# Softmax attention on one core: a new order of the hand-written word lists, with the next batch's K sums later and one V load moved

## The chip, the cores and the metric

The kernel runs on one core of one Trainium2 chip. The metric is the device time of one execution in microseconds. Three runs of the kernel before took 792.56, 793.68 and 793.29, with a median of 793.29. The profile is of one more execution of the same program.

Engines are called by the names of the profile: PE is TensorE's matmuls, PEld its weight loads, DVE is VectorE, ACT ScalarE, POOL GpSimd and SP SyncE. POOL and SP only issue transfers here.

## The reference

```python
batch, seq_len, d_model = 8, 2048, 512
scores = np.matmul(q, k.transpose(0, 2, 1)) / np.sqrt(d_model)
attn_weights = special.softmax(scores, axis=-1).astype(np.float32)
return np.matmul(attn_weights, v)
```

All inputs and the output are float32. The kernel computes in float16 with float32 accumulation.

## The kernel before

**Two stages, both with seven products in place of eight.** Each batch has 2048 queries in two superblocks of 1024, and 2048 keys in 16 blocks, taken as 8 pairs `j`. For a superblock and a pair the 2 x 2 block product K times Q is made with Strassen's scheme (the Winograd form): seven products instead of eight, at the price of sums of the operands. Such a unit is a score *group* (class Group, lines 266 to 330). It is numbered through the whole kernel, so that group 48 is the first of the seventh superblock. Product n of a group is two matmuls of 512 columns. After it, ScalarE or VectorE empties or adds the bank: product 1 is copied to a second bank (L308), 5 and 6 are copied to SBUF (L312, L315), 7 and 3 are added there (L318, L321), 4 and 2 go through the exponential (L237). A further exponential takes the SBUF tile (the word `e`). The second stage multiplies the weights with V in the same way: a *pair* product (class Pair, L494) is eight matmuls of 256 or 257 columns, and a *leaf* product (class Leaf, L418) goes one level deeper, with eight matmuls of 128 columns, whose result VectorE adds to the output rows at once (L426).

**Sums.** VectorE makes the sums of operands: of K in `k_sums` (L185 to L188, four instructions for half a batch's keys), of Q in `q_sums` (L202 to L205), of V (L219 to L222 and L376 to L379), and of the weights (L352 to L355 for pairs, L395 to L398 for leaves). In K the second sum overwrites the raw block a21.

**The order is written by hand.** The kernel runs through 32 periods, four to a batch. A period is one string of words in `SEQUENCES` (lines 589 to 629), and each word issues its instructions on their engines at that place. Every engine takes its own instructions strictly in the order in which the words issue them, and waits at an instruction until its operands and its room are there. Periods 0, 1, 30 and 31 have strings of their own (`first`, `second`, `alone`, `last`); the others use the string of their number modulo 4, here called kind 0, 1, 2 and 3. Period 9 is thus of kind 1 and period 10 of kind 2. Kind 0 opens a batch of the second stage and kind 3 closes it. The score stage runs two periods ahead: kinds 0 and 1 score the batch's second superblock, and kinds 2 and 3 the next batch's first.

The words, with `'` for the period before:

- `.` is the next score product. QORDER (line 586) interleaves two groups: product 1 of this group, 7 of the one before, 5, 6, then 4 of the one before, 3, 2. `e` is the exponential of a finished SBUF tile.
- `a1` to `b7` are pair products of the tiles a and b; `L1` to `L7` are leaf products, of which L3 and L4 also scale and store rows (L435, L440 on SP).
- `xa0` to `xa3` are weight sums for the a tile of the next period, `xb0` to `xb3` for b of this one, and `ya0` to `ya3` the rest of a sum begun a period earlier (the last two of eight pairs in kind 2). `s1` to `s4` are leaf sums.
- `K00` is sum 0 of the next batch's first half of K, `K10`, `K20`, `K30` its sums 1 to 3; `K01` to `K31` are of the second half. `q0` to `q3` are sums of Q; `V..` of V, `w` and `u` of V's leaves.
- `lk2`, `lq3`, `lv1` load a chunk of K, Q or V of the next batch (POOL queue); `tk2`, `tq3` transpose a loaded chunk of K or Q by a transfer (SP queue, L146). Loads of K and Q share two stage buffers.

For the change these ties matter. K00 (into `ks1`) reads what tk0 and tk1 brought; its reader is product 5 of the next batch's first group (group 48 for periods 9 and 10). K20 is read by that group's product 6, K30 by product 3, K10 by product 7. q0 and q1 are read by products 5 and 6. The score banks are few: two for product 1 (`qx`), one each for its copy (`qy`) and for product 5 (`qz`); product 1 of a group takes the bank that product 4 of the group two before has left, once ScalarE has read it. One bank (`py`) serves the leaf products.

Of the kernel before, what the change touches and what calls it, by code (L numbers as in the profile page):

```python
# [12 lines left out]
def kernel(  # L13
# [561 lines left out]
    def pv(g, which):  # L575
# [3 lines left out]
        if which[1] == "1" and which[-1] != ">":  # L579
# [9 lines left out]
    SEQUENCES = {  # L589
        'first': (  # L590
# [4 lines left out]
        ),  # L595
# [4 lines left out]
        ),  # L600
# [4 lines left out]
        ),  # L605
# [4 lines left out]
        ),  # L610
        3: (
            "K11' a1 . . xa3' b7' . a5 xb0 . . L5' . e . L6' . s4' . . L3' s3' . . . L7' xb1 e xb2 "
            "xb3 a3 . . . b1 a6 e . . . a7 L4' s1 b5 xa0 . . L2 . s2 . . q0 xa1 L1 . . xa3 . . xa2 b3 "
            "q2 e q1 "
        ),
# [5 lines left out]
        ),  # L621
        'alone': (
# [1 line left out]
            "L4' xb2 a6 b3 xa2 a2 a7 b6 xa1 a4 xa3 b2 "  # L624
        ),
        'last': (
            "b7' q0 a1 a5 xb0 xb1 b4' a3 xb3 b1 b5 a6 b3 a2 xb2 b2 q1 b6 a7 b7 a4 q2 b4 "
        ),
    }

# [254 lines left out]
```

## Time and profile before

| what | value |
|---|---|
| median of three runs | 793.29 us |
| the profiled execution, own time | 789.77 us |
| its span, first to last instruction | 788.0 us |
| granted TensorE clock | 1.000 |
| busy share of the span: PE, DVE, ACT, POOL | 99%, 87%, 77%, 9% |
| DVE busy in periods 9, 10, 11, 12 | 21.57 of 24.00, 21.26 of 24.00, 19.00 of 23.90, 24.12 of 24.20 us |
| HBM traffic | 100.70 MB read, 33.55 MB written |
| one sum of 128 x 1024 in float16 on DVE | 0.68 us |
| a load of V, issue to landing, median | 9.8 us |

How to read it: all times inside the profile are counted from the span's start. A row of the timeline gives the start, the duration, the engine, the line of the kernel, the operation and its tiles; in brackets stands how long the engine was idle before, and what ended that. Matmuls overlap: a row's duration runs to the end of its pipeline, and the next may start before. What tells whether TensorE stands still is therefore the distance between starts.

### The profile page before, as it was taken

The page shows a single profiled execution, that of the slowest core. Times are in us where ns is not written, and L with a number is a line of the kernel's source. Part 1 is how long each engine was busy: PE and PEld are TensorE (multiplying, and loading weights), DVE is VectorE, ACT ScalarE, POOL GpSimd, SP SyncE. Part 2 cuts the span into 40 slices and gives each one's busy share as a digit, 9 for nine tenths or more (in the row PEclk, how much of TensorE's full clock was granted, in tenths as well). Part 3 has the DMA queues.
Part 4 walks back from the last instruction along what each step waited for, and adds up shares of the span by engine and source line. Part 5 has one row for each costly group of instructions (what it writes and reads, how often), then busy time and mean ns, then how long its engine had stood idle before and what let it go on. Part 6 is the DMA issues. An engine that isn't in the chain of part 4 may idle for free.

```text
span 788.0 us, 16301 instructions
## 1 busy us (share of the span) xinstructions
PE 783.1 (99%) x6284; PEld 536.5 (68%) x6284; DVE 685.4 (87%) x1452; ACT 610.4 (77%) x1140; POOL 71.7 (9%) x104
## 2 busy tenths in 40 slices
PE   9999999999999999999999999999999999999998
PEld 6566767667666666666766666666666766766687
DVE  5799988989889888998879988799897989889884
ACT  4888778787877878878787877878778787787762
POOL 4011100011000110010100001000110002000000
PEclk9999999999999999999999999999999999999999
DMA  9999995889958898489984989859996789911113
GB/s 220 183 167 133 183 188 110 166 145 164 180 120 162 155 172 166 97 161 180 170 158 110 159 161 183 160 103 174 155 203 123 124 172 147 202 54 46 48 66 111
DMA packets 187773, 115.90 MB, mean 147 GB/s; under 512 B 121520, under 2 KB 170800, under 8 KB 187696
## 3 DMA queue, kind: packets, MB, share of 16 engines
q0 software_dynamic: 49648, 49.29, 43.8%
q1 hardware_dynamic: 137616, 65.22, 36.1%
q8 instruction: 49, 0.80, 0.4%
q10 hardware_dynamic: 432, 0.36, 0.1%
q14 instruction: 28, 0.23, 0.1%
HBM read 100.70 MB, written 33.55 MB: 170 GB/s over the span
## 4 chain that ended last, share of the span: by engine, by line
PE 99%; DMA 0%; DVE 0%; issue 0%
PE t L298 47%; PE t L494 36%; PE t L418 12%; PE t L243 1%; PE t L258 1%; PE tr L156 1%; DMA rows<-in_q_dram 0%; PE t L768 0%; PE t L566 0%; DVE kraw L159 0%; DVE stage L135 0%; DVE rows L506 0%
## 5 line engine op out<-in xcount | busy, mean ns | idle before, releaser
L298 PE MATMUL t<-qraw,kraw 128*128 128x512 f16 x732 | 194.7, 379 | 0.0
L494 PEld LDWEIGHTS <-s 128*128 128x128 f16 x1536 | 148.3, 98 | 42.4 <-ACT rows L503 0.3
L298 PEld LDWEIGHTS <-kraw 128*128 128x128 f16 x984 | 93.0, 98 | 72.8 <-issue 0.3
L298 PE MATMUL t<-qs,ks 128*128 128x512 f16 x492 | 140.0, 379 | 0.0
L494 PE MATMUL t<-vt,s 128*128 128x257 f16 (+1 forms) x1024 | 132.9, 273 | 0.0
L237 ACT ACTIVATE right<-cz 128x1024 f16<-128x1024 f32 x123 | 130.1, 1058 | 1.9 <-DVE cz L318 1.9
L503 ACT ACTIVATE rows<-t,scales 128x256 f32<-128x256 f32 x136 | 63.9, 471 | 51.5 <-DVE scales L528 19.2
L426 DVE TENSOR_TENSOR rows<-t,rows 128x256 f32<-128x256 f32 x210 | 88.3, 420 | 15.5 <-PE t L418 8.1
L298 PEld LDWEIGHTS <-ks 128*128 128x128 f16 x738 | 68.7, 98 | 46.5 <-issue 0.4
L321 DVE TENSOR_TENSOR cz<-t,cz 128x512 f32<-128x512 f32 x123 | 84.4, 686 | 11.0 <-ACT cz L315 6.4
L237 ACT ACTIVATE left<-t 128x512 f16<-128x512 f32 x128 | 76.7, 600 | 20.2 <-PE t L298 16.4
L506 DVE SCALAR_TENSOR_TENSOR rows<-t,scales,rows 128x256 f32<-128x256 f32 (+1 forms) x134 | 63.9, 479 | 30.1 <-ACT rows L503 17.2
L318 DVE TENSOR_TENSOR cz<-t,cz 128x512 f32<-128x512 f32 x123 | 84.2, 684 | 5.1 <-PE t L298 5.1
L237 ACT ACTIVATE right<-t 128x512 f16<-128x512 f32 x138 | 83.0, 604 | 5.5 <-PE t L298 3.0
L312 ACT COPY cz<-t 128x512 f32<-128x512 f32 x122 | 71.5, 586 | 10.0 <-PE t L298 8.1
L315 ACT COPY cz<-t 128x512 f32<-128x512 f32 x123 | 71.8, 584 | 8.5 <-PE t L298 8.3
L418 PEld LDWEIGHTS <-left 128*128 128x128 f16 x960 | 62.6, 98 | 23.2 <-DVE left L398 3.8
L308 ACT COPY t<-t 128x512 f32<-128x512 f32 x121 | 69.8, 577 | 6.5 <-PE t L298 4.1
L298 PE MATMUL t<-qraw,ks 128*128 128x512 f16 x246 | 73.2, 379 | 0.0
L298 PE MATMUL t<-qs,kraw 128*128 128x512 f16 x246 | 73.2, 379 | 0.0
L494 PE MATMUL t<-vh,right 128*128 128x256 f16 x544 | 69.8, 273 | 0.0
L494 PEld LDWEIGHTS <-right 128*128 128x128 f16 x568 | 55.5, 98 | 17.5
(87 smaller groups left out, 1078.7 us busy)
## 6 DMA issues: line engine op xcount, KB each, us to landing
out_dram<-rows SPq DMA_DIRECT2D x60, 512.0 KB, 3.5
vh<-in_v_dram POOLq DMA_DIRECT2D x32, 512.0 KB, 9.8
stage<-in_q_dram POOLq DMA_DIRECT2D x28, 512.0 KB, 7.8
stage<-in_k_dram POOLq DMA_DIRECT2D x28, 512.0 KB, 6.7
right<-in_k_dram POOLq DMA_DIRECT2D x3, 512.0 KB, 11.8
out_dram<-rows SPq DMA_DIRECT2D x4, 256.0 KB, 2.0
out_dram<-rows SPq DMA_DIRECT2D x7, 128.0 KB, 1.7
rows<-in_q_dram SPq DMA_DIRECT2D x2, 256.0 KB, 3.2
```

The source lines that it names most:

```text
L237: nc.scalar.activation(out=out_, in_=in_, func=EXP, scale=inv_sqrt_d)
L298: nc.tensor.matmul(dst[:], lhs[:, j, dc, :], rhs[:, :, dc, :], start=(n in (1, 5) and dc == 0), stop=(dc == 1), skip_group_check=True,)
L308: self.edges[0](out=self.y[:], in_=self.x[:])
L312: self.edges[1](out=self.cz[:, 1, :], in_=self.z[:])
L315: nc.scalar.copy(out=self.cz[:, 0, :], in_=self.x[:])
L318: nc.vector.tensor_add(self.cz[:, 1, :], self.x[:], self.cz[:, 1, :])
L321: nc.vector.tensor_add(self.cz[:, 0, :], self.z[:], self.cz[:, 0, :])
L418: nc.tensor.matmul(to, lhs[:, j, h, :], rhs[:, j, :], start=(n in (1, 2) and h == 0 and j == 0), stop=(j == NK - 1), skip_group_check=True,)
L426: nc.vector.tensor_add(acc, part, acc)
L494: nc.tensor.matmul(dst[:, 0:width], lhs(j), rhs(j), start=(first and j == 0), stop=(j == NJ - 1), skip_group_check=True,)
L503: nc.scalar.activation(out=out_, in_=src, func=COPY, scale=r)
L506: nc.vector.scalar_tensor_tensor(out=out_, in0=src, scalar=r, in1=out_, op0=MULT, op1=ADD)
```

## The change

Only strings of `SEQUENCES` change; no instruction is added or taken away. In kind 1, K00, K20 and K30 move towards the end, and a7 and the products around it change places. The word `lv2` moves from kind 2, behind lq2, to the sixth place of kind 3, behind lv3. In kind 2, tk3 and tq3 are issued later, lq2 earlier in the string, and xb3, K01, K21, K31, q3, ya3, a3, b1 and L4' change places. Kinds 3 and 0, `first` and `last` have small exchanges of neighbours.

```diff
         'first': (
...
-            "za1 a5 v33 za3 . xb0 . . a3 v22 xb2 v21 . . lk0 v30 za2 . a6 . . v31 v32 xb1 tq1 . a7 . "
+            "za1 a5 v33 za3 . xb0 . . a3 v22 xb2 v21 . . lk0 v30 za2 . a6 . . v31 v32 xb1 . a7 tq1 . "
...
         1: (
             "a1 w3' . b7' . . L6' . w2' s4' . e L5' . . . s3' L3' a5 lk3 . xb0 xb1 . e . L7' xb3 . "
-            "tk1 a3 . . . xb2 a6 L4' . . . lk2 b1 . s1 K00 e K20 s2 a7 tk2 . lv1 . . L2 . b5 xa0 L1 . "
-            "q0 xa1 xa3 xa2 e . K30 . . b3 q2 q1 b6 . "
+            "tk1 a3 . . . xb2 a6 L4' . a7 lk2 . . b1 L2 . s1 e s2 . lv1 . . . b5 tk2 xa0 K00 . q0 K20 "
+            "L1 xa1 xa2 e . . b3 . q1 b6 . xa3 q2 K30 "
         ),
         2: (
-            ". . . b7' e K10' . L5' ya0 ya1 . tk3 . lq2 a1 lv2 . a5 ya3 q3 s3' L6' . . s4' ya2 . xb0 "
-            "e a3 . . L3' . xb1 xb2 a6 L7' K01 . lq3 tq3 K21 . a7 b1 xb3 . . . L4' b5 . L2 . s1 xa0 . "
-            "b3 xa2 e lv3 . tq2 K31 . s2 . b6 xa1 . L1 . . . e "
+            ". . . b7' e K10' . L5' ya0 ya1 lq2 a1 . tk3 . . a5 q3 ya3 s3' L6' . . s4' ya2 a3 . xb0 e "
+            ". . L3' . b1 xb1 xb2 a6 L7' xb3 K01 . lq3 . . . a7 L4' b5 K21 . . s1 xa0 tq3 . . L2 b3 "
+            "xa2 e lv3 . tq2 . s2 . b6 xa1 . L1 K31 . . . e "
         ),
         3: (
-            "K11' a1 . . xa3' b7' . a5 xb0 . . L5' . e . L6' . s4' . . L3' s3' . . . L7' xb1 e xb2 "
-            "xb3 a3 . . . b1 a6 e . . . a7 L4' s1 b5 xa0 . . L2 . s2 . . q0 xa1 L1 . . xa3 . . xa2 b3 "
-            "q2 e q1 "
+            "K11' a1 . . xa3' lv2 . a5 xb0 b7' . . L5' . e . L6' . s4' . . L3' s3' . . . L7' xb1 e "
+            "xb2 xb3 a3 . . . b1 a6 e . . . a7 L4' s1 b5 xa0 . . L2 . s2 . . xa1 L1 . q0 . xa3 . . "
+            "xa2 b3 q2 e q1 "
         ),
         0: (
...
-            "lk0 e L3' q3 xb1 V11 a3 . V21 . . xb2 L7' V31 lq1 V20 b1 . . . lv0 . V30 a6 ya2 . xb3 . "
-            "w0 u0 tk0 e . . L4' b5 xa0 w1 a7 u1 s1 . . u2 lk1 xa1 L2 . u3 b3 . xa3 b6 . . s2 L1 . e "
+            "lk0 e L3' q3 xb1 V11 a3 . V21 . xb2 . L7' V31 lq1 V20 b1 . . . lv0 . V30 a6 ya2 . xb3 . "
+            "w0 u0 tk0 e . . L4' b5 xa0 a7 u1 s1 . . u2 lk1 xa1 . L2 u3 b3 . w1 xa3 b6 . . L1 s2 . e "
             "xa2 tq1 "
         ),
...
         'last': (
-            "b7' q0 a1 a5 xb0 xb1 b4' a3 xb3 b1 b5 a6 b3 a2 xb2 b2 q1 b6 a7 b7 a4 q2 b4 "
+            "q0 b7' a1 a5 xb0 xb1 b4' xb3 a3 b1 b5 a6 b3 xb2 b2 a2 q1 b6 a7 b7 a4 q2 b4 "
         ),
```

## The prediction, as it was put on record

> **What bounds the kernel.** I read the totals first, then what TensorE waited for, then four periods of one batch side by side, then VectorE's waits, and last the places where a sum of K and the product that needs it stand in time.
>
> ```profile
> PE 783.1 (99%) x6284; PEld 536.5 (68%) x6284; DVE 685.4 (87%) x1452; ACT 610.4 (77%) x1140; POOL 71.7 (9%) x104
> ```
> ```profile
> PE t L768 <- DVE vt L709: 1.2, 1, 1.2
> PE t L258 <- DVE kraw L159: 0.2, 1, 0.2
> ```
> ```profile
> 252.10:276.10 24.00, 24.00 (x193) 16.41 (x192) 21.57 (x44) 19.72 (x37) 2.23 (x3) 1.00 0.87 154
> 276.10:300.10 24.00, 24.00 (x194) 16.42 (x193) 21.26 (x47) 18.76 (x36) 2.97 (x4) 1.00 1.05 165
> ```
>
> The first fence is the page's totals, the second all that the list of waits has for TensorE (both in the opening), the third periods 9 and 10 (columns: stretch, its length, then busy time of PE, PEld, DVE, ACT, POOL, granted clock, DMA share, GB/s). TensorE (PE) is busy for all 24.00 us of both, at clock 1.00. VectorE (DVE) has 2.4 and 2.7 us to spare in a period.
>
> A score product (two matmuls) is followed 0.43 us later by the next product, eight matmuls of 256 columns 0.88 us later, a leaf product 0.45 us later. Taking the start of every matmul in the trace against these distances, all excess after the opening (from 20 us on) is nine gaps of 0.03 to 0.14 us, **0.77 us in sum**. Nothing that only reorders work can win more than that from this execution: instruction counts do not change, and every product still has to be issued. The rest is the opening, which the change does not touch, and some 3 us after the last matmul.
>
> The time of the profiled execution is 789.77 (span 788.0 and 1.8 around it); the median shown is 793.29, so 3.5 us more. No view says where those 3.5 us are. I carry the difference over unchanged, and come back to it under the rivals.
>
> **Sums of K, kind 1 (periods 5, 9, ... 25).** The change takes K00 and K20 from behind s1 and puts them behind xa0 and q0; K30 becomes the period's last sum. VectorE does the same 0.68 to 0.69 us for each.
>
> ```profile
> DVE ks L185 <- DMA kraw<-stage: 2.2, 3, 0.9
> ```
> ```profile
> 172.47 0.69 DVE L185 TENSOR_TENSOR ks<-kraw 128x1024 f16<-128x1024 f16 x1 [0.94 <-DMA kraw<-stage]
> ...
> 175.40 0.42 DVE L426 TENSOR_TENSOR rows<-t,rows 128x256 f32<-128x256 f32 x1
> ```
> ```profile
> 174.90 1.04 PE L494 MATMUL t<-vt,s 128*128 128x257 f16 x8
> 175.87 0.38 PE L418 MATMUL t<-vh,right 128*128 128x128 f16 x4
> ```
> ```profile
> 164.77 5.50 SPq L146 DMA_TRANSPOSE kraw<-stage  x1
> ```
>
> K00 (L185) waited for K's transpose in three periods, 2.2 us in sum. In period 5 the wait of 0.94 pushed all of VectorE's queue back: the leaf add at 175.40 ended at 175.82, and the next leaf product, which uses the same bank, came 0.97 us after the product before it instead of 0.88. So 0.94 us of wait cost TensorE **0.09 us**; in the other two (0.42 and 0.85) there was no gap. The slack behind this wait is thus about 0.85 us.
>
> Where does K00 start afterwards? In front of b5 stand the same products before and after (eight scores, a7, b1 and L2 after L4', in another order), so b5 starts at 270.88 in period 9 as now, its reciprocal runs 271.96 to 272.13, xa0 ends at 272.59, K00 runs 272.51 to 273.19: 5.1 us later than its 267.42. The transpose had landed by 266.4, when the next load into its buffer was issued. In period 5, 95.97 us earlier, K00 would start near 176.5, 4 us after the landing. So the wait goes: gain 0.09 us, and a cover of 4 us where there was none.
>
> What is late next? The rows behind K00 now:
>
> ```profile
> 276.85 0.68 DVE L203 TENSOR_TENSOR qs<-qraw,qs 128x1024 f16<-128x1024 f16 x1
> ```
> ```profile
> 276.98 0.59 PE L298 MATMUL t<-qs,ks 128*128 128x512 f16 x2
> 277.41 1.04 PE L494 MATMUL t<-vh,right 128*128 128x256 f16 x8
> 278.29 0.59 PE L298 MATMUL t<-qs,ks 128*128 128x512 f16 x2
> ```
>
> Product 5 of the next batch's first group (276.98) reads K00's and q0's sums, product 6 (278.29) K20's and q1's. Today q1 (L203) ends at 277.53, 0.76 us ahead. I went through VectorE's queue in the new order with the durations above, each instruction starting at the end of the one before or of its operand. K00 ends at 273.19, q0 at 273.8, K20 at 274.4: 3 to 4 us ahead of their products. Then L1's add, xa1, xa2, a recip and an add, and q1 ends at 276.9: 1.4 us ahead, better than today. Then b6's add, xa3, q2, and K30 ends at 279.0. Product 3, its reader, stands behind a1 in the new kind 2, at 279.60 + 0.88 = 280.48: 1.5 us ahead, where it was 3.9. VectorE enters period 10 with 1.0 us more in arrears (b7's add at 279.5 instead of 278.49). It was idle 0.46 and 0.83 us by 282.4, waiting for ScalarE and for a5, so the debt is gone there. Cost: nothing; without that idle time it would be up to 1.0 us in each of 7 batches.
>
> **TensorE's order in kind 1** brings one new close place. Product 4 of group 45 comes at 265.23 + 0.43 + 0.88 + 0.87 + 0.88 + 0.45 = 268.73, ends at 269.33, ScalarE's exponential of it (0.60) at 269.97, and the product 1 that takes its bank is due at 268.73 + 3 x 0.432 = 270.03. That leaves **0.06 us**, where it was 0.59. ScalarE is free by then (b1's copy ends at 268.86), so I take nothing; bounds 0 to 0.14 us a batch, by the largest gap of the trace.
>
> **Kinds 2, 3 and 0.** K01 and K21 move behind xb3 (they have 12.6 and 13.2 us), K31 to the end (4.7 left of 7.4), q3 goes ahead of ya3, w1 and s2 go later in kind 0. The closest edges stay those of now: 0.06 us (s4' to L3' in kind 3), 0.04 to 0.09 us (kind 0). Nothing, within 0 to 0.14 us a period.
>
> **Queues.** SP: the transposes tk2 and tk3 are issued where they are released, tk2 by its load (273.40), tk3 by product 4 of group 47, which a1 now pushes from 279.2 to 280.1: 0.9 us later, and the load of Q chunk 3 with it. K01 follows K's landing by 3 us as now. The store of L4' now stands ahead of tq3 instead of behind its wait (298.5 in period 10), which frees rows earlier; no one waited for it. POOL: the load lv2 no longer goes at 281.38 but behind lv3, which went at 287.33 and comes up to 0.9 later. Nothing in POOL's queue holds it back there, so it is issued at 288 to 289, in the same period after all. Loads of V take 9.8 us; V01 reads it 38 us later. Nothing. The swap of tq1 in the first period and those in the last two, no instruction more or less, are under 0.1 us either way.
>
> **Sum.** 788.0 - 0.1 = 787.9 for the span (bounds -0.8 and +2.0, below), and 793.29 - 0.1 = **793.2 us**. About 0.2%, 1.6 us, is what a measurement can tell from no change.
>
> A rule speaks against reading 99% as full. The Trainium skill (Perfetto Trace Analysis, Identifying the Most-Contended Engine) says that busy matmul time is a bad measure and that weight-load time shows the headroom. By it 32% of the span, an estimated 251 us, would be open. Here no product in the steady part follows another sooner than the distances above, so I do not take it; it has 1 in 100, among the faster.
>
> **Rivals.**
> - *The timed runs hold waits that the profile does not show (faster, 0.24).* For: they are 3.5 us longer, differ by 1.1 us, and K's transpose lands 12.7 to 15.4 us after the period's first score product within this one execution, against 0.85 us of slack. If it lands 0.5 us later still, each of 7 batches loses about 0.5 us, which is all of the 3.5. Against: a constant offset explains the same. Half of it recovered gives 791.5, all of it 789.8.
> - *The new close places miss (slower, 0.13).* Product 4 to product 1 in kind 1, with its 0.06 us, and VectorE's arrears at the start of kind 2 (ya0 ends 0.24 us ahead of a5, 0.67 now). It decides once ScalarE or VectorE is later there than these margins. Two misses a batch at the largest gap, 0.144 us: 2 x 7 x 0.144 = 2.0, so 795.2. Against: both are tied to TensorE's own ends, not to a DMA.
> - *The change does not do what it says.* For lv2 this holds (POOL runs ahead, above); it costs nothing and is part of the forecast.
>
> **Numbers.** No measurable change 0.62, faster 0.25 (0.24 and 0.01), slower 0.13. The likeliest case alone spans 792.4 to 793.9. The range goes down to 790.9, over most of the first rival, and up to 794.6, small misses; about 0.07 and 0.13 are left out.
>
> **What would show it.** Right: no wait of L185 for K's transpose; L203 ends over 1 us before its product; VectorE's totals as now; TensorE without gaps in all periods. Wrong: gaps of TensorE ahead of product 1 in kind 1 that ScalarE releases, or ahead of a5 in kind 2 that VectorE releases (slower); a median 1.6 us lower while the two profiles have the same span (the timed runs hid waits).

## The result, and the profile after

The changed kernel takes **789.58 us** (median of six runs, 789.30 to 790.24), the kernel before, run beside it, 793.16 (six runs, 792.56 to 794.08). The ratio is 0.9956, 95% interval 0.9943 to 0.9968: 3.6 us faster. The ratios in this document lie near the ratio of the mean times, not of the medians, and leave out an execution over 1.5% above the fastest of its kernel. The forecast was 793.2 with a range down to 790.9. The result lies under that range, close to the 789.8 that the first rival gave for its case "all of it".

The two profiled executions differ by far less: 789.77 before, 789.34 after, spans 788.0 and 787.6. So nearly all of the gain is in what the profile of before did not show.

The totals of after, and its stretches for periods 9 and 10 (length, busy time of PE, PEld, DVE, ACT, POOL, granted clock, DMA share, GB/s):

```profile
PE 782.2 (99%) x6284; PEld 535.9 (68%) x6284; DVE 683.8 (87%) x1452; ACT 610.6 (78%) x1140; POOL 71.6 (9%) x104
```
```profile
252.10:276.10 24.00, 24.00 (x194) 16.46 (x193) 20.17 (x42) 19.99 (x37) 2.23 (x3) 1.00 0.93 161
276.10:300.10 24.00, 24.00 (x194) 16.43 (x193) 21.92 (x48) 18.41 (x36) 2.97 (x4) 1.00 0.89 154
```

Nothing here tells the kernels apart: TensorE is full in both stretches; VectorE works 1.40 us less in period 9 than before, and 0.66 us more in period 10. The excess of TensorE's matmul distances after the opening is 0.22 us (before 0.77). Three of the gaps that are gone (0.13, 0.07 and 0.14 us, at 308.05, 523.46 and 525.79 before) stand in the second profile of the kernel before too (run 1), and in neither profile of the changed kernel: 0.34 us of the gain, for which the prediction took nothing. In the list of waits L185 no longer stands.

The sums around the border of periods 9 and 10 stand where the walk through VectorE's queue had put them (timeline of after, VectorE, then TensorE):

```profile
272.47 0.68 DVE L185 TENSOR_TENSOR ks<-kraw 128x1024 f16<-128x1024 f16 x1
...
276.21 0.68 DVE L203 TENSOR_TENSOR qs<-qraw,qs 128x1024 f16<-128x1024 f16 x1
...
278.27 0.68 DVE L188 TENSOR_TENSOR ks<-kraw,ks 128x1024 f16<-128x1024 f16 x1
```
```profile
276.95 0.59 PE L298 MATMUL t<-qs,ks 128*128 128x512 f16 x2
...
278.25 0.59 PE L298 MATMUL t<-qs,ks 128*128 128x512 f16 x2
...
280.44 0.59 PE L298 MATMUL t<-qraw,ks 128*128 128x512 f16 x2
```

K00 starts at 272.47 (forecast 272.51), q1 ends at 276.89, 1.36 us ahead of product 6 (forecast 1.4), K30 ends at 278.95, 1.49 ahead of product 3 (forecast 1.5).

### The profile page after: what moved, and what is told of

It is laid out like the page before. It is cut to its first block, busy times and chain, and to the rows that moved or that the text cites. A ratio compares the mean times of both kernels' runs of the same rounds, so it can differ in the third digit from the quotient of the medians.

```text
span 787.6 us, 16286 instructions
## 1 busy us (share of the span) xinstructions
PE 782.2 (99%) x6284; PEld 535.9 (68%) x6284; DVE 683.8 (87%) x1452; ACT 610.6 (78%) x1140; POOL 71.6 (9%) x104
## 4 chain that ended last, share of the span: by engine, by line
PE 98%; DMA 2%; POOL 0%; ACTq 0%; DVE 0%; issue 0%
PE t L298 47%; PE t L494 36%; PE t L418 12%; PE t L243 1%; DMA right<-in_k_dram 1%; DMA rows<-in_k_dram 1%; PE tr L156 0%; PE t L258 0%; POOL right L121 0%; PE t L566 0%; ACTq L95 0%; POOL gate L728 0%; DVE rows L506 0%
## 5 line engine op out<-in xcount | busy, mean ns | idle before, releaser
L298 PE MATMUL t<-qraw,kraw 128*128 128x512 f16 x732 | 192.4, 379 | 0.0
L318 DVE TENSOR_TENSOR cz<-t,cz 128x512 f32<-128x512 f32 x123 | 84.2, 684 | 4.5 <-PE t L298 3.8
L494 PE MATMUL t<-vh,s 128*128 128x257 f16 x512 | 66.7, 273 | 0.0
## 6 DMA issues: line engine op xcount, KB each, us to landing
vh<-in_v_dram POOLq DMA_DIRECT2D x32, 512.0 KB, 10.7
```

The source lines that it names most:

```text
L298: nc.tensor.matmul(dst[:], lhs[:, j, dc, :], rhs[:, :, dc, :], start=(n in (1, 5) and dc == 0), stop=(dc == 1), skip_group_check=True,)
L318: nc.vector.tensor_add(self.cz[:, 1, :], self.x[:], self.cz[:, 1, :])
L494: nc.tensor.matmul(dst[:, 0:width], lhs(j), rhs(j), start=(first and j == 0), stop=(j == NJ - 1), skip_group_check=True,)
```

## Where the time was: the experiments

Each run of before was made beside the kernel it is compared with, on the chip of that comparison; the comparisons used several chips. "Gap" is what a distance between two matmul starts exceeds its usual value by, as in the prediction. When I name the *late transpose*, I mean this theory, which the first run gave: in kind 2, sum K01 (L185) waits for tk3, the transpose of K's chunk 3 (L146), and behind K01 wait VectorE's next instructions, then product 4.

**1. The kernel before once more.** No edit.

> The kernel before, unchanged, to get a second profile of it. Its timed runs took 3.4 us longer than its one profiled execution (793.16 against 789.77). All three theories expect 793.2 and a span near 791 if this execution is like the timed ones, with about 3 us of gaps between TensorE's starts after the opening, where the first profile had 0.77. K theory: the gaps lie in kind 1, behind K00 (L185) waiting over 0.85 us for K's transpose, about 0.4 to 0.6 us in each of 6 batches. V theory: they lie in kinds 2 and 3, where a transpose or the sum K01 waits for a load that stands behind lv2. Order theory: they lie at several places where VectorE or ScalarE is late without any transfer. If this execution is again a short one (span 788), nothing is told apart.

Measured: 791.12 (median of 10, 789.83 to 792.50) against 791.12 (35 runs, 789.59 to 796.97), ratio 0.9999 [0.9983, 1.0015]. The profiled execution took 791.53 this time, span 789.8: 1.8 us longer than the first profile of the same program. First batch, period 2 of the *first* profile (SP's queue, POOL's, VectorE, TensorE):

```profile
83.33 6.63 SPq L146 DMA_TRANSPOSE kraw<-stage  x2
```
```profile
88.84 0.74 POOL L121 DMA_DIRECT2D stage<-in_q_dram  x1 [11.74 <-DMA kraw<-stage]
89.57 0.75 POOL L211 DMA_DIRECT2D vh<-in_v_dram  x1
```
```profile
97.51 0.68 DVE L185 TENSOR_TENSOR ks<-kraw 128x1024 f16<-128x1024 f16 x1
...
99.83 0.68 DVE L318 TENSOR_TENSOR cz<-t,cz 128x512 f32<-128x512 f32 x1
```
```profile
100.38 1.04 PE L494 MATMUL t<-vt,s 128*128 128x257 f16 x8
101.26 0.59 PE L298 MATMUL t<-qs,kraw 128*128 128x512 f16 x2
```

and the same place in the *second*:

```profile
79.95 15.43 SPq L146 DMA_TRANSPOSE kraw<-stage  x2
```
```profile
88.10 0.74 POOL L121 DMA_DIRECT2D stage<-in_q_dram  x1 [12.79 <-DMA kraw<-stage]
88.83 0.75 POOL L211 DMA_DIRECT2D vh<-in_v_dram  x1
```
```profile
100.11 0.69 DVE L185 TENSOR_TENSOR ks<-kraw 128x1024 f16<-128x1024 f16 x1 [2.05 <-DMA kraw<-stage]
...
102.44 0.68 DVE L318 TENSOR_TENSOR cz<-t,cz 128x512 f32<-128x512 f32 x1
```
```profile
100.85 1.04 PE L494 MATMUL t<-vt,s 128*128 128x257 f16 x8
103.18 0.59 PE L298 MATMUL t<-qs,kraw 128*128 128x512 f16 x2 [1.28 <-DVE cz L318]
```

The chain reads as follows. K01 waits 2.05 us for the transpose. L318, which empties product 7's bank, stands behind K01 and ends at 103.12. Product 4 takes that bank and starts at 103.18, 2.33 us after the product before it instead of 0.88: a gap of 1.45 us. In the first profile L318 ended at 100.51, 0.75 us ahead of product 4. This gap is most of the 1.8 us; another 0.47 us passed in the opening, where a score product that started at 47.18 in the first profile started at 47.65.

Why was the transpose late? The SP row joins tk2 and tk3. In the first profile tk3 went at 87.92 and landed at 94.16, after 6.24 us; the loads lq2 (L121) and lv2 (L211) were issued behind it. In the second lq2 went at 88.10, ahead of tk3 at 88.39, which landed at 100.02, after 11.62 us. Two things race here: POOL's lq2 is released by the landing of tk2, tk3 by a product of TensorE.

**2. The new places of K in kind 1 alone**, TensorE's order as before.

```diff
-... L4' . . . lk2 b1 . s1 K00 e K20 s2 a7 tk2 . lv1 . . L2 . b5 xa0 L1 . q0 xa1 xa3 xa2 e . K30 . . b3 q2 q1 b6 .
+... L4' . . . lk2 b1 . s1 e s2 a7 tk2 . lv1 . . L2 . b5 xa0 K00 L1 . q0 K20 xa1 xa3 xa2 e . . . b3 q1 q2 K30 b6 .
```

> The kernel before with K00, K20 and K30 alone moved (K00 behind xa0, K20 behind q0, K30 behind q1 and q2), TensorE's order and all transfers as before. K theory: 789.6 to 790.2, the whole gain, and no wait of L185. V theory and order theory: 792.9 to 793.4, as before.

Measured: 797.73 (794.14 to 801.15), ratio 1.0077 [1.0054, 1.0099], so slower. K00's wait is gone, but VectorE now enters kind 2 in arrears: gaps of 0.13 + 0.22 + 0.26 = 0.61 us at its first products (those starting at 182.85, 183.94 and 185.07 in the second batch), in the six batches behind the first one, 3.6 us in sum. They also push tk3's release back, and four of seven transposes took 10.6 to 13.5 us, with gaps of 0.47, 3.35, 0.49 and 0.74 us at product 4. List of waits:

```profile
DVE ks L185 <- DMA kraw<-stage: 7.4, 4, 4.0
```

So this part does not carry the gain by itself. In the change TensorE's order moves with it, and none of these gaps is there.

**3. The move of lv2 alone** (`lq2 a1 lv2 . a5` in kind 2 becomes `lq2 a1 . a5`, and `xa3' b7'` in kind 3 becomes `xa3' lv2 b7'`).

> The kernel before with lv2 alone moved to kind 3, behind lv3 in the queue of loads. V theory: 789.6 to 790.2. K theory and order theory: 792.9 to 793.4, and L185 still waits for K's transpose in some batches.

Measured: 790.27 (789.60 to 795.45), ratio 0.9991 [0.9969, 1.0013]: no difference by the interval, the median 0.85 us lower. In its profile six of tk3's transfers took 5.9 to 7.9 us, one 10.33, with a gap of 0.15 us.

**4. Meant as the change with kind 1 put back; it was not.** By my mistake only the string `first` was put back (tq1 ahead of a7). The expectation speaks of another kernel.

> The changed kernel with the string of kind 1 as it was before (K00 and K20 early, TensorE's old order there); all else as changed. K theory: 792.9 to 793.4, the gain gone, waits of L185. V theory: 789.6 to 790.2, the gain kept. Order theory: between, by the share of kind 1 in it.

Measured: 789.47 (788.98 to 791.17), ratio 0.9980 [0.9965, 0.9995]. It shows only that the swap in the first period is worth nothing measurable.

**5. The change with kind 1's string truly put back.**

> The changed kernel with the string of kind 1 as it was before (K00 and K20 early, TensorE's old order there); the rest as changed. Transfer theory (the timed runs lose their time in kind 2, where the sum K01 waits for the transpose tk3, which is slow when the loads lq2 and lv2 start ahead of it): the gain stays, 789.3 to 789.9, and L185 may wait up to 1 us for tk1 without a gap of TensorE over 0.1 us. K00 theory (they lose it in kind 1, behind K00): the gain is gone, the level of the kernel before on this chip (791 to 793).

Measured: 790.03 (789.10 to 793.94) against 791.15 (35 runs), ratio 0.9990 [0.9975, 1.0005]. No wait at K01. In the first batch K00 waited 1.30 us for tk1, with gaps of 0.37 and 0.25 us behind it. But that batch's K00 stands in period 1, whose string `second` is the same in both kernels. In the six periods of kind 1 no K00 waited (tk1 landed 0.21 to 1.74 us ahead), and there was no gap behind one. So a cost of the old kind 1 does not show in this profile; why the median is 0.6 us above that of the changed kernel (789.45 in run 10, on another chip) stays open.

**6. The change with lv2 put back** behind lq2 in kind 2.

> The changed kernel with lv2 back behind lq2 in kind 2; the rest as changed. Transfer theory: a1 ahead of product 4 of the old group lets tk3 go only behind lq2 and lv2 in nearly every batch, so tk3 takes 10 to 13 us instead of 6 to 8, K01 waits 1 to 4 us in most batches, and the time is 792 to 800, slower than before. K00 theory: 789.3 to 789.9, as the changed kernel.

Measured: 792.36 (789.97 to 794.86), ratio 1.0018 [1.0001, 1.0034]: the gain is gone, and slightly more. Timeline of the worst batch, VectorE and TensorE:

```profile
292.97 0.69 DVE L185 TENSOR_TENSOR ks<-kraw 128x1024 f16<-128x1024 f16 x1 [2.47 <-DMA kraw<-stage]
293.58 0.68 DVE L318 TENSOR_TENSOR cz<-t,cz 128x512 f32<-128x512 f32 x1
```
```profile
292.76 0.59 PE L298 MATMUL t<-qs,ks 128*128 128x512 f16 x2
294.32 0.59 PE L298 MATMUL t<-qs,kraw 128*128 128x512 f16 x2 [0.96 <-DVE cz L318]
```

The same chain in the new order: 1.56 us between two products where 0.43 is usual. K01 waited in four batches, 6.4 us in sum.

**7. The kernel before with only K01, K21 and K31 later in kind 2**; no transfer and no product moved.

```diff
-... L7' K01 . lq3 tq3 K21 . a7 b1 xb3 . . . L4' b5 . L2 . s1 xa0 . b3 xa2 e lv3 . tq2 K31 . s2 . b6 xa1 . L1 . . . e
+... L7' . lq3 tq3 . a7 b1 xb3 . . . L4' b5 K01 K21 . L2 . s1 xa0 . b3 xa2 e lv3 . tq2 . s2 . b6 xa1 . L1 K31 . . . e
```

> The kernel before with K01 and K21 moved behind b5 and K31 behind L1 in kind 2 (K01 near 293.4 in period 10 instead of 289.4, still 10 us ahead of its reader); every transfer and TensorE's order as before. Transfer theory: the landing of tk3 has 4 us more to come in, so 789.3 to 790.0, nearly the whole gain without touching a transfer; tk3 itself stays as slow as it is. K00 theory: as before on this chip (791 to 793).

Measured: 789.66 (11 of 12 between 789.35 and 790.50, one 794.97), ratio 0.9990 [0.9973, 1.0008], the median 1.5 us under the 791.15 beside it. In its profile two transposes took 10.06 and 10.78 us and cost nothing, because K01 came 2.8 us or more after every landing. The interval holds 1, since the one execution of 794.97, of which there is no trace, weighs on the mean. Eleven of the twelve are at or under 790.50, and of the kernel before beside it 14 of 35.

**8. A third load put beside the two** (lv3 moved in front, behind lv2, in the kernel before).

> The kernel before with lv3 moved up beside lv2, so that three loads (lq2, lv2, lv3) start around tk3 instead of two. Transfer theory: where tk3 starts behind them it takes 12 to 17 us, and the time is 1 to 6 us above the kernel before; where it starts ahead of them nothing changes. K00 theory: as before.

Measured: 796.17 (788.95 to 803.63), ratio 1.0028 [1.0000, 1.0056]. The profiled execution, the longest, took 803.63. Two of its transposes, with lq2 first, took 15.03 and 14.85 us; the other five, with tk3 ahead, took 4.3 to 6.8. Rows of the first batch, and stretches around it:

```profile
104.21 0.69 DVE L185 TENSOR_TENSOR ks<-kraw 128x1024 f16<-128x1024 f16 x1 [5.45 <-DMA kraw<-stage]
```
```profile
107.27 0.68 PE L298 MATMUL t<-qs,kraw 128*128 128x512 f16 x2 [4.68 <-DVE cz L318]
...
108.60 1.06 PE L298 MATMUL t<-qraw,ks 128*128 128x512 f16 x2
```
```profile
96.00:102.00 6.00, 6.00 (x56) 4.51 (x54) 2.68 (x6) 2.60 (x6) 0.00 (x0) 1.00 1.36 202
102.00:108.00 6.00, 1.32 (x11) 0.82 (x9) 3.38 (x7) 1.95 (x6) 0.75 (x1) 0.97 0.70 134
108.00:114.00 6.00, 6.00 (x36) 3.73 (x35) 4.49 (x9) 4.11 (x9) 0.00 (x0) 0.75 0.79 148
```

The twelve times fall into three groups: five from 788.95 to 792.02, six from 796.11 to 796.90, and the 803.63. In the trace each of the two late transposes cost 6.5 and 6.3 us in sum, the slow stretch behind the gap included. That is the step between the groups, so they read as no late transpose, one and two; only the last execution has a trace.

**9 and 10. The change with K01 and K21 still later** (both behind b5), and **the change itself again**.

> The changed kernel with K01 and K21 moved on, behind b5 (K01 near 293.0 in period 10 instead of 290.5). A version that should beat both if any does. Transfer theory: every wait of K01 goes, 5 us of cover instead of 2 to 3, so the slower runs of the changed kernel (up to 791.2) go as well: median 789.2 to 789.5, all runs but the odd one under 790. The floor is TensorE's own work, so the median can win 0.3 us at most. K00 theory: no difference from the changed kernel.

> The changed kernel itself, beside the others on the same chip. 789.3 to 789.7 by both theories; the profile shows tk3 at 6 to 8 us, 10 at most, and K01 waiting under 1 us.

Measured: 789.46 (788.91 to 789.78), ratio 0.9970 [0.9954, 0.9985], and 789.45 (788.96 to 791.17), ratio 0.9971 [0.9954, 0.9988], against 791.42 (24 runs). In the changed kernel one transpose of seven took 10.04 us and K01 waited 0.35 us, with no gap. The version with K01 later has no wait and no execution above 789.8; its median is the same. It is the best one here, by its spread only.

**11. lv2 and K01 together, first try.** Its kernel is not what its expectation says: lv2 moved, but K01 went behind L2 and the score word after it, K21 behind xa0, and K31 stayed.

> The kernel before with only two parts: lv2 moved behind lv3 into kind 3, and K01, K21 (behind b5) and K31 (behind L1) later in kind 2. Kind 1 as before. Transfer theory: 789.2 to 789.8, the whole gain of the change. K00 theory: 791 to 793, as before.

Measured: 796.54, ratio 1.0077 [1.0050, 1.0104]. No sum waits for a transfer, yet product 4 has a gap of 0.93 us or more in every batch, 6.8 us in sum:

```profile
PE t L298 <- DVE cz L318: 5.6, 7, 1.0
```

Here K01 itself comes too late for TensorE. The sums have a window with two ends.

**12. lv2 and K01 together, as meant** (the edits of 3 and 7 in the kernel before).

> The kernel before with two things alone: lv2 moved to kind 3 (xa3' lv2 b7'), and in kind 2 K01 and K21 put behind b5 and K31 behind L1, as in the run that moved these sums alone. It replaces the run in which K01 stood too far back. Theory of the late transpose (the time is lost where sum K01 waits for the transfer tk3, which takes 10 us and more when loads start ahead of it): both halves of the remedy are there, so no wait of L185 for kraw in kind 2, tk3 mostly at 4 to 8 us with single ones near 10, no gap over 0.15 us at product 4 behind b6, 789.2 to 789.9 us, within 0.5 us of the changed kernel, and no execution above 791.5. Theory of K00 (the time was lost at tk1 and K00 in kind 1, which stays as before): 791 to 793. If VectorE's queue were too late even so: gaps of about 0.9 us at product 4 in every batch, 795 or more.

Measured: 790.15 (789.41 to 791.39) against 791.89 (17 runs, 789.67 to 800.74), ratio 0.9971 [0.9949, 0.9993]. The time lies between the two theories, and the trace says why (VectorE, TensorE):

```profile
269.58 0.69 DVE L185 TENSOR_TENSOR ks<-kraw 128x1024 f16<-128x1024 f16 x1 [2.25 <-DMA kraw<-stage]
...
272.51 0.41 DVE L426 TENSOR_TENSOR rows<-t,rows 128x256 f32<-128x256 f32 x1
```
```profile
270.71 1.04 PE L494 MATMUL t<-vt,s 128*128 128x257 f16 x8
272.98 0.38 PE L418 MATMUL t<-vh,right 128*128 128x128 f16 x4 [1.23 <-DVE rows L426]
```

This is K00 in kind 1. tk1 was issued at 260.58 as in the first profile (260.75) but landed at 269.49 instead of 265.84; the load lk3 had gone only 1.1 us ahead of it (259.43), in the first profile 4.6 us (256.16). K00 waited 2.25 us, and the leaf product behind it came 1.39 us late, which bears out the slack of 0.85 us that the prediction had read off. So the place that the prediction had named does cost time too, in some batches.

**The race in all 98 batches.** In the fourteen traces, of seven batches each, tk3's time from issue to landing sorts by its lead over lq2:

| loads beside tk3 | lead of tk3 over lq2 | batches | tk3, issue to landing |
|---|---|---|---|
| lq2 and lv2 | over 0.5 us | 27 | 4.25 to 7.1 us |
| lq2 and lv2 | 0.29 us | 1 | 8.5 us |
| lq2 and lv2 | under 0.2 us, or behind | 12 | 9.5 to 13.5 us |
| lq2, lv2 and lv3 | behind | 2 | 14.9 and 15.0 us |
| lq2 alone | over 0.2 us | 38 | 4.3 to 8.3 us |
| lq2 alone | 0.0 to 0.2 us | 4 | 10.0 to 10.7 us |
| lq2 alone | behind | 14 | 6.0 to 7.9 us |

(The other five batches with lv3 had a lead of over 1.1 us and stand in the first row: 4.3 to 6.8 us.) In the kernel before, K01 stands some 9.6 us after tk3's issue (279.79 to 289.38 in period 10), with 0.6 us of slack behind it (a wait of 2.05 us made a gap of 1.45 in run 1, one of 0.75 a gap of 0.15 in run 3). In the changed kernel tk3 goes 0.84 us later and K01 0.95 us later (280.63, 290.33), so K01's move gives the transpose no more time; but waits of 0.35 and 0.61 us made no gap there (runs 10 and 4). The cases with both loads in front reach past this, those with lq2 alone hardly do.

**The gaps account for the times.** In all fourteen traces the span is the same sum: the start of one score product at the end of the opening (the 337th matmul, ahead of every edit, at 47.07 to 48.46 us), the gaps behind it (0.11 to 13.27 us, slow stretches included) and 740.2 us, to within 0.05 us. So nothing else on TensorE tells these executions apart. The opening, which no edit touches, moves by up to 1.4 us from execution to execution.

## Why the prediction was wrong

- **"No view says where those 3.5 us are. I carry the difference over unchanged."** This step failed. The difference was no constant: span and time differ by 1.8 us in both kernels' profiled executions, and in the later comparisons, where spans are recorded, before's longer executions have longer spans. The one profile was a lucky execution, with all seven transposes ahead of their loads. Of the 111 executions of the kernel before in the later comparisons, 11 took no longer than its 789.77.
- **"K01 follows K's landing by 3 us as now"** and **lv2: "Nothing"**. Both edits were costed at nothing by a margin read off that one execution (2.7 to 5.7 us in its seven batches). They carry most of the gain. With lv2 put back the ratio is 1.0018 in place of 0.9971 (runs 6 and 10, on different chips), and K01 moved alone takes 1.5 us off the median. In the kernel before the two together, with K01 further back than the change puts it, give 0.9971 [0.9949, 0.9993] (run 12), as much as the whole change made again in run 10. I looked at lv2 only for its own reader, V01, and not at what its transfer does to the transpose beside it.
- **The rival "the timed runs hold waits that the profile does not show"** was right in sign, and its 789.8 is close, but it stood at 0.24 and at the wrong place. It put the loss at tk1 and K00, about 0.5 us in each of seven batches. In the eight traces with kind 1 as before, K00 waited there in 7 of 48 batches, and two of the waits made a gap: 0.09 us in the first profile and 1.39 us in run 12. The larger part was one period later, at tk3 and K01, which showed no wait at all in the first profile, and it comes as single batches that lose, 1.45 us in run 1. The size was in part luck: in run 10 the same change won 2.0 us, not 3.6.
- **"The new close places miss"** did not happen: no gap at the place with 0.06 us of slack, none ahead of a5. Run 2 shows that the arrears meant there are real when only the sums move: 0.61 us a batch, where the prediction had 2 x 0.144.
- **lv2 goes behind lv3** was right. POOL ran ahead and issued both together (timeline of after):

```profile
288.45 0.74 POOL L121 DMA_DIRECT2D stage<-in_q_dram  x1 [7.93 <-DMA kraw<-stage]
289.19 1.50 POOL L211 DMA_DIRECT2D vh<-in_v_dram  x2
```

  But that it is issued "in the same period after all" did not make it worthless: lq3, the load in front of it (L121), waits for tk3's landing, at 287.92 here, so lv2, some 8 us later than before, meets tk3 in no batch.
- **The rule on weight loads** as headroom: weight loads are busy 68% in after as in before, and no execution of the changed kernel went under 788.96. The trace decides against it.

Left open: which batches lost the race in the runs of the first comparison, since only times are recorded there; before's median was 793.2 in it and 791.1 to 791.9 in the later ones. Why the lead decides so sharply is not shown either. The Trainium skill (DMA: Bandwidth & Descriptors, Queues, rings and completion order) says that each DMA engine takes turns between the queues it has work for, a packet at a time. That agrees with a transpose slowed by loads, and with 15 us for three of them; it does not tell why lq2 alone, when it comes up to 0.2 us behind tk3, is worse (10.0 to 10.7 us) than when it is ahead (6.0 to 7.9).

## What to carry to other kernels

When a kernel's timed runs are longer than its profiled one by more than what lies around the span, profile it again before reasoning: a hand-ordered schedule can hold races between transfers that one execution happens to win. List each sum that reads a transfer with its margin to the landing, and ask what the same transfer would take if a neighbouring load went first. A moved load is costed by the transfers that it leaves alone or meets, not only by its own reader.

## What was not expected of the hardware

- The same transpose tk3 took 4.25 us at best, and 9.5 to 13.5 us when two loads of 512 KB, issued 0.7 us apart, began ahead of it or less than 0.2 us behind it.
- After a long gap TensorE ran at half rate. In run 8 the gap was 4.85 us; then two matmuls of 512 columns took 0.85 us start to start (108.60 to 109.45) instead of 0.43, and the distances were doubled from 107.7 to 111.1, for 3.4 us; the granted clock of the stretch 108 to 114 is 0.75. Its second gap, of 4.67 us, did the same, and so did one of 3.35 us in run 2:

```profile
390.00:396.00 6.00, 2.89 (x25) 1.91 (x23) 2.95 (x6) 1.14 (x4) 1.48 (x2) 1.00 0.43 108
396.00:402.00 6.00, 5.92 (x32) 3.49 (x32) 4.10 (x11) 4.31 (x9) 0.00 (x0) 0.72 1.23 210
```

  Gaps of up to 1.45 us had no such effect. A late transpose can thus cost more than its wait: 4.85 us became 6.5. The Trainium skill (TensorE: Matmul & The Clock Gate, Part 1: The HAM clock gate) gives half clock after an idle window of about 3.4 us and full clock after as long a busy one. The trace agrees with both, as far as three gaps can show; none here lies between 1.45 and 3.35 us.
